# Transposing the next batch's K and Q in 512-column units, one unit per query tile, in a hard-max attention kernel

## The chip, the cores and the metric

The kernel runs on one core of one Trainium2 chip. The metric is the time of one execution on the device in microseconds (us). Every kernel here was executed several times; unless said otherwise a time is the median of those executions, with the lowest and the highest beside it. Times are compared only between executions of the same chip session and only between executions in the fast state.

The engines are named by what they do: TensorE multiplies matrices (PE in the profile, PEld for its weight loads), VectorE (DVE) does elementwise work and reductions, ScalarE (ACT) here moves results from PSUM, the memory that this kernel's matmuls write, to SBUF, where its other tiles lie (such a move is called an eviction below), GpSimd (POOL) issues gathers.

## The reference

For each of four batches, every query picks the key with the largest dot product and returns that key's row of V. There is no softmax.

```python
B, Sq, Sk, D = 4, 4096, 4096, 128        # q, k, v: float32 normal numbers

def reference(q, k, v):
    logits = np.matmul(q, k.transpose(0, 2, 1))
    best = np.argmax(logits, axis=-1)
    b_idx = np.arange(q.shape[0])[:, None]
    return v[b_idx, best, :].astype(np.float32)
```

## The kernel before

A query tile is 128 queries; there are 32 tiles a batch, 128 in all. For each tile the kernel screens groups of four keys in fp16 with a mix of sums and differences (max(a, b) = half of the sum plus half of the absolute difference), then recomputes the best groups exactly. Only the screening matters here. A tile costs:

- TensorE: 12 matmuls of 512 columns: two `pd` tiles (differences) of two, two `psn` tiles (sums) of two, and two more per `psn` that add the absolute difference `A`.
- ScalarE: three evictions of 1024 columns: `A` twice, `E` once.
- VectorE: the fold (an int16 maximum of `psn` and `E` into `W`), the top-8 search of `W`, and small work.

```python
    pp = ctx.enter_context(tc.tile_pool(name="ps", bufs=4, space=bass.MemoryType.PSUM))
    # ... cut: the four slots of this pool hold all PSUM tiles, up to 1024 fp32 columns each
    def dpart(t, x):
        # ... cut
        ps = pp.tile([P, 1024], FP32, tag="u", name=f"pd_{t}_{x}")
        mm(ps, t, 1 + 2 * x, True)
        A = ep.tile([P, 1024], FP16, tag=f"A{x}", name=f"A_{t}_{x}")
        nc.scalar.activation(out=A, in_=ps, func=AF.Abs)

    def spart(t, x):
        # ... cut
        ps = pp.tile([P, 1024], FP32, tag="u", name=f"psn_{t}_{x}")
        mm(ps, t, 2 * x, False)
        # ... cut: adds A with two matmuls by an identity
        if x == 0:
            E = ep.tile([P, 1024], I16, tag="E", name=f"E_{t}")
            nc.scalar.activation(out=E, in_=ps, func=AF.Relu)
        # ... cut: the second psn stays in PSUM for the fold

    def fold(t):
        E, ps = E_t.pop(t)
        nc.vector.tensor_tensor(out=W_t[t % NW].bitcast(I16)[:, 1::2], in0=ps, in1=E, op=OP.max)
```

While a batch runs, the K and Q of the next batch are loaded in natural order and transposed on TensorE. Each block of 1024 columns is transposed into one PSUM tile and evicted by ScalarE in one instruction. A block of K takes 16 matmuls of 128 columns, since each output is a sum or a difference of two keys' columns. A block of Q takes 8.

```python
    def trn_half(b, u, h):
        x = 2 * (u // 2)
        if h == 0:
            tk_t[u] = pp.tile([P, 1024], FP32, tag="u", name=f"tk_{b}_{u}")
        ps = tk_t[u]
        for m in range(4):
            o = ps[:, h * 512 + m:(h + 1) * 512:4]
            nc.tensor.matmul(out=o, lhsT=natk[b % 2][:, h, 4 * m + x, :], rhs=identh, start=True, stop=False)
            nc.tensor.matmul(out=o, lhsT=natk[b % 2][:, h, 4 * m + x + 1, :],
                             rhs=identn if u % 2 else identh, start=False, stop=True)
        if h == 1:
            nc.scalar.activation(out=kT[b % 2][:, u * 1024:(u + 1) * 1024], in_=ps, func=AF.Copy)
    # ... cut: trn_k calls trn_half for h = 0 and 1; trn_q is the same for Q, 8 matmuls, adjacent columns

        # the loop over tiles; qt is the tile's number in its batch
            if 2 <= qt < 10:
                load_part(b + 1, qt - 2)          # K of the next batch
            elif 14 <= qt < 22:
                load_part(b + 1, qt - 6)          # Q of the next batch
            if 18 <= qt < 22:
                trn_k(b + 1, order[qt - 18])      # one K block in each of four tiles
            if 24 <= qt < 24 + NQT // 8:
                trn_q(b + 1, qt - 24)             # one Q block in each of four tiles
            # ... cut
            if it > 0:
                screen(it)
        if 0 <= it - 1 < T:
            fold(it - 1)
        if it % NQT in (9, 13) and it < T:
            put_k(it // NQT + 1, it % NQT // 13)  # a VectorE instruction of 0.94 us, twice a batch
```

## Time and profile before

| | before |
|---|---|
| time, median of 3 (range) | 505.31 us (504.83 to 505.49) |
| profiled execution | 510.92 us, span 508.9 us |
| VectorE / TensorE / ScalarE busy | 419.9 / 402.2 / 390.3 us |
| tile with no transposes | 3.1 us |
| tile with a K block | 3.9 to 4.9 us (exceptions: 2.9 us for the first in batches 0 and 2, 5.4 us for one with flag work) |
| tile with a Q block | 3.3 to 3.7 us |

The profiled execution took 5.6 us longer than the median of the timed ones. (Flag work is a chain of short VectorE and TensorE instructions, run once for each half of the tiles, that looks for queries that need a further exact check.)

First, the page of the kernel before: the span, the busy time of each engine with its share and count, and three groups of instructions. A group's line gives busy time and mean ns of one, then the engine's idle time just before these instructions and what ended most of it.

```profile
span 508.9 us, 6436 instructions
PE 402.2 (79%) x1960; PEld 188.6 (37%) x1960; DVE 419.9 (83%) x833; ACT 390.3 (77%) x417; POOL 312.8 (61%) x345
L211 DVE TENSOR_TENSOR W<-psn,E 128x1024 int16<-128x1024 f32 x128 | 166.3, 1299 | 33.7 <-ACT E L198 23.7
L153 ACT ACTIVATE kT<-tk 128x1024 f16<-128x1024 f32 x16 | 16.3, 1026 | 23.7 <-PE tk L150 22.6
L167 ACT ACTIVATE qT<-tq 128x1024 f16<-128x1024 f32 x16 | 18.5, 1159 | 0.7 <-PE tq L165 0.7
```

VectorE is the busiest, but 83% does not say whether it is the limit. The fold line says that VectorE stood idle for 33.7 us before folds, mostly for `E` from ScalarE (10.5 us of this lie ahead of the program's first fold). The kT line says that ScalarE in turn stood idle for 23.7 us before the K evictions, waiting for the transposes.

Next, busy time by stage in the same trace: a stretch of the last batch, the K tiles of the second batch (numbered batch 1 from here on), and that batch's Q tiles.

```profile
core 0: us, PE busy (x) PEld busy (x) DVE busy (x) ACT busy (x) POOL busy (x), PEclk, DMA share, GB/s
380.00:440.00 60.00, 48.48 (x204) 19.64 (x203) 60.00 (x122) 47.86 (x51) 38.12 (x39) 0.97 0.26 74
175.00:194.00 19.00, 18.10 (x110) 11.15 (x109) 13.26 (x25) 14.91 (x16) 13.53 (x15) 1.00 0.63 108
194.00:214.00 20.00, 18.70 (x105) 8.88 (x104) 18.34 (x34) 20.00 (x24) 11.39 (x13) 1.00 0.28 67
```

Where there is nothing to transpose, VectorE is busy for all of 60.00 us, so it is the limit. In the K tiles no engine is busy all the time: VectorE 13.26 of 19 us, ScalarE 14.91, but TensorE 18.10. TensorE's own work in a K tile is 12 x 0.215 + 16 x 0.109 = 4.32 us, which is most of the tile; the rest points to a chain of waits. In the Q tiles ScalarE is busy for all of 20.00 us.

The chain in a K tile is seen on ScalarE's timeline (start, duration, then in brackets its idle time before and what ended it):

```profile
180.76 1.02 ACT L153 ACTIVATE kT<-tk 128x1024 f16<-128x1024 f32 x1 [1.08 <-issue]
181.68 1.02 ACT L185 ACTIVATE A<-pd 128x1024 f16<-128x1024 f32 x1
182.58 1.03 ACT L198 ACTIVATE E<-psn 128x1024 int16<-128x1024 f32 x1
183.49 1.04 ACT L185 ACTIVATE A<-pd 128x1024 f16<-128x1024 f32 x1
185.60 1.02 ACT L153 ACTIVATE kT<-tk 128x1024 f16<-128x1024 f32 x1 [1.08 <-PE tk L150]
```

ScalarE does four evictions about 0.905 us apart, then waits 1.08 us for the next block's transposes. 4 x 0.905 + 1.08 = 4.7 us, and the tile takes 4.84 us (185.60 - 180.76). VectorE, which needs 3.1 us, waits for the rest before its folds:

```profile
179.03 1.31 DVE L211 TENSOR_TENSOR W<-psn,E 128x1024 int16<-128x1024 f32 x1 [1.00 <-PE psn L195]
183.88 1.31 DVE L211 TENSOR_TENSOR W<-psn,E 128x1024 int16<-128x1024 f32 x1 [1.46 <-PE psn L195]
188.72 1.30 DVE L211 TENSOR_TENSOR W<-psn,E 128x1024 int16<-128x1024 f32 x1 [1.92 <-ACT E L198]
193.29 1.31 DVE L211 TENSOR_TENSOR W<-psn,E 128x1024 int16<-128x1024 f32 x1 [1.36 <-ACT E L198]
```

### The profile page before, as it was taken

The numbers are of one execution on the slowest core, as the hardware profiler recorded it, in microseconds if no ns is written. First come the engines' busy times: TensorE is split into PE (matmuls) and PEld (weight loads), VectorE is DVE, ScalarE is ACT, GpSimd is POOL, SyncE is SP. The second block draws the span as 40 slices with busy tenths as digits, with TensorE's granted clock in tenths as the row PEclk, the third lists the DMA queues.
The fourth block names the chain that finished last, engine by engine and source line by source line (L and its number), as shares of the span: only waits on it lengthen the run. The fifth ranks groups of instructions, "written<-read, shape, count | busy, mean of one in ns | idle before, by whom it ended". The sixth has DMA issues, their size and how long they took to land. (4 is left out here: it accounts for less than half of the span.)

```text
span 508.9 us, 6436 instructions
## 1 busy us (share of the span) xinstructions
PE 402.2 (79%) x1960; PEld 188.6 (37%) x1960; DVE 419.9 (83%) x833; ACT 390.3 (77%) x417; POOL 312.8 (61%) x345
## 2 busy tenths in 40 slices
PE   8999999999999799999998899999988999000000
PEld 5544455444433364444333644443333333000000
DVE  2179997999999968999999889999999999861030
ACT  1999978999998779999998699999978999000000
POOL 9124456556787876566887865576646666677430
PEclk9999999999999999999999999999999999655555
DMA  9715254232545572314554651323311313244210
GB/s 133 126 24 90 83 77 66 59 88 61 124 90 148 109 129 55 93 52 107 96 131 118 102 104 50 84 62 91 98 37 57 96 55 101 58 117 114 73 55 4
DMA packets 51751, 43.47 MB, mean 85 GB/s; under 512 B 24424, under 2 KB 45931, under 8 KB 51712
## 3 DMA queue, kind: packets, MB, share of 16 engines
q0 software_dynamic: 31520, 30.97, 30.5%
q1 hardware_dynamic: 20192, 12.06, 8.1%
q8 instruction: 15, 0.25, 0.2%
q14 instruction: 24, 0.20, 0.1%
HBM read 39.59 MB, written 12.19 MB: 102 GB/s over the span
## 5 line engine op out<-in xcount | busy, mean ns | idle before, releaser
L185 ACT ACTIVATE A<-pd 128x1024 f16<-128x1024 f32 x256 | 266.9, 1106 | 8.6 <-PE pd L176 6.7
L231 POOL DMA_INDIRECT kg<-k,cand x128 | 125.7, 982 | 128.0 <-DVE p L250 34.2
L211 DVE TENSOR_TENSOR W<-psn,E 128x1024 int16<-128x1024 f32 x128 | 166.3, 1299 | 33.7 <-ACT E L198 23.7
L176 PE MATMUL psn<-kT,qT 128*128 128x512 f16 x512 | 151.8, 378 | 23.5 <-ACT A L185 12.6
L176 PEld LDWEIGHTS <-qT 128*128 128x128 f16 x1024 | 100.0, 98 | 171.2 <-issue 79.6
L176 PE MATMUL pd<-kT,qT 128*128 128x512 f16 x512 | 152.5, 379 | 6.6 <-ACT A L185 3.0
L214 DVE MAX8 TOP<-W 128x8 f32<-128x1024 f32 x128 | 156.0, 1219 | 0.0
L195 PE MATMUL psn<-A,identh 128*128 128x512 f16 x512 | 152.1, 378 | 0.0
L281 POOL DMA_INDIRECT vr<-in_v_dram,win x128 | 126.8, 991 | 39.0 <-issue 37.2
L198 ACT ACTIVATE E<-psn 128x1024 int16<-128x1024 f32 x128 | 141.1, 1102 | 9.4 <-PE psn L195 4.1
L195 PEld LDWEIGHTS <-identh 128*128 128x128 f16 x512 | 49.6, 97 | 60.8
L246 DVE TENSOR_TENSOR prod<-kg,natq 128x768 f16<-128x768 f16 (+1 forms) x65 | 35.1, 541 | 3.0 <-DMA kg<-k,cand 3.0
L153 ACT ACTIVATE kT<-tk 128x1024 f16<-128x1024 f32 x16 | 16.3, 1026 | 23.7 <-PE tk L150 22.6
L149 PE MATMUL tk<-identh,natk 128*128 128x128 f16 x128 | 28.7, 309 | 0.2 <-issue 0.2
L250 DVE TENSOR_TENSOR p<-prod 128x384 f16<-128x384 f16 (+1 forms) x65 | 22.5, 348 | 0.0
L65 POOL DMA_DIRECT2D natq<-in_q_dram x26 | 22.3, 857 | 0.1
L255 DVE TENSOR_REDUCE D<-p 128x6 f32<-128x192 f16 (+1 forms) x65 | 21.6, 333 | 0.0
L336 PE MATMUL fp<-n,tri 128*128 128x1 f32 x4 | 0.9, 304 | 24.1 <-DVE n L332 24.1
L167 ACT ACTIVATE qT<-tq 128x1024 f16<-128x1024 f32 x16 | 18.5, 1159 | 0.7 <-PE tq L165 0.7
L150 PEld LDWEIGHTS <-natk 128*128 128x128 f16 x128 | 17.2, 134 | 2.0 <-issue 0.8
L149 PEld LDWEIGHTS <-natk 128*128 128x128 f16 x128 | 17.3, 135 | 1.5
L62 POOL DMA_DIRECT2D natk<-in_k_dram x26 | 15.7, 604 | 0.9 <-POOLq L605 0.8
(87 smaller groups left out, 168.7 us busy)
## 6 DMA issues: line engine op xcount, KB each, us to landing
out_dram<-vr SPq DMA_DIRECT2D x13, 512.0 KB
k<-kd SPq DMA_DIRECT2D x8, 384.0 KB
natk<-in_k_dram POOLq DMA_DIRECT2D x24, 128.0 KB
natq<-in_q_dram POOLq DMA_DIRECT2D x24, 128.0 KB
kg<-k,cand POOLq DMA_INDIRECT x128
vr<-in_v_dram,win POOLq DMA_INDIRECT x128
natk<-in_k_dram POOLq DMA_DIRECT2D x2, 512.0 KB
out_dram<-vr SPq DMA_DIRECT2D x4, 256.0 KB
```

The costliest lines, as they stand in the source:

```text
L65: nc.gpsimd.dma_start(out=natq[b % 2][:, x:y], in_=q[b].rearrange("(t p) d -> p t d", p=P)[:, x:y])
L149: nc.tensor.matmul(out=o, lhsT=natk[b % 2][:, h, 4 * m + x, :], rhs=identh, start=True, stop=False)
L176: nc.tensor.matmul(out=ps[:, n * 512:(n + 1) * 512], lhsT=qT[b % 2][:, qt * P:(qt + 1) * P], rhs=kT[b % 2][:, u * 1024 + n * 512:u * 1024 ...
L185: nc.scalar.activation(out=A, in_=ps, func=AF.Abs)
L195: nc.tensor.matmul(out=ps[:, n * 512:(n + 1) * 512], lhsT=identh, rhs=A[:, n * 512:(n + 1) * 512], start=False, stop=True)
L198: nc.scalar.activation(out=E, in_=ps, func=AF.Relu)
L211: nc.vector.tensor_tensor(out=W_t[t % NW].bitcast(I16)[:, 1::2], in0=ps, in1=E, op=OP.max)
L214: nc.vector.max(out=TOP[:, t, :], in_=W_t[t % NW].bitcast(FP32))
L231: near_q.append(lambda j=j: nc.gpsimd.indirect_dma_start(out=kg[:, j].rearrange("p f d -> p (f d)"), out_offset=None, in_=k16[t0 // NQT], ...
L246: nc.vector.tensor_tensor(out=prod, in0=kg, in1=natq[b % 2][:, x - b * NQT:x - b * NQT + m, :].unsqueeze(2).to_broadcast([P, m, 3, P]), op ...
L250: nc.vector.tensor_tensor(out=p1, in0=prod[:, :, :, 0:64], in1=prod[:, :, :, 64:128], op=OP.add)
L281: late_q.append(lambda j=j: nc.gpsimd.indirect_dma_start(out=vr[:, j, :], out_offset=None, in_=v_flat, in_offset=IOA(ap=win[:, j:j + 1], a ...
```

## The change

The intent: cut the eight blocks of a batch into 16 units of 512 columns, each with its own PSUM tile and its own eviction, and give each of 16 consecutive tiles one unit (K in tiles 10 to 17, Q in 18 to 25). ScalarE then never waits for 16 transposes at once, and no tile carries a full fourth eviction. The arithmetic and the number of matmuls stay the same; 24 evictions are added. The Q loads move two tiles earlier. The first batch's own transposes at the start stay as they were.

```diff
--- before.py
+++ after.py
@@ -152,10 +152,22 @@
         if h == 1:
             nc.scalar.activation(out=kT[b % 2][:, u * 1024:(u + 1) * 1024], in_=ps, func=AF.Copy)
 
-    def trn_k(b, u):
-        if b < B:
-            trn_half(b, u, 0)
-            trn_half(b, u, 1)
+    def unit_k(b, u, h):
+        x = 2 * (u // 2)
+        ps = pp.tile([P, 512], FP32, tag="u", name=f"uk_{b}_{u}_{h}")
+        for m in range(4):
+            o = ps[:, m::4]
+            nc.tensor.matmul(out=o, lhsT=natk[b % 2][:, h, 4 * m + x, :], rhs=identh, start=True, stop=False)
+            nc.tensor.matmul(out=o, lhsT=natk[b % 2][:, h, 4 * m + x + 1, :],
+                             rhs=identn if u % 2 else identh, start=False, stop=True)
+        nc.scalar.activation(out=kT[b % 2][:, u * 1024 + h * 512:u * 1024 + (h + 1) * 512], in_=ps, func=AF.Copy)
+
+    def unit_q(b, g):
+        ps = pp.tile([P, 512], FP32, tag="u", name=f"uq_{b}_{g}")
+        for i in range(4):
+            nc.tensor.matmul(out=ps[:, i * P:(i + 1) * P], lhsT=natq[b % 2][:, g * 4 + i, :], rhs=identh,
+                             start=True, stop=True)
+        nc.scalar.activation(out=qT[b % 2][:, g * 512:(g + 1) * 512], in_=ps, func=AF.Copy, scale=QSCALE)
 
     def trn_q(b, g):
         if b >= B:
@@ -482,7 +494,6 @@
     cuts = list(range(0, T - 24 + 1, 8)) + [T - x for x in (20, 16, 12, 8, 6, 4, 2, 1, 0)]
     chunks = list(zip(cuts[:-1], cuts[1:]))
     SEGS = [0, T // 2, T]
-    order = (1, 0, 3, 2)
     live = []
 
     def start(g, kind):
@@ -550,12 +561,13 @@
             b, qt = it // NQT, it % NQT
             if 2 <= qt < 10:
                 load_part(b + 1, qt - 2)
-            elif 14 <= qt < 22:
-                load_part(b + 1, qt - 6)
-            if 18 <= qt < 22:
-                trn_k(b + 1, order[qt - 18])
-            if 24 <= qt < 24 + NQT // 8:
-                trn_q(b + 1, qt - 24)
+            elif 12 <= qt < 20:
+                load_part(b + 1, qt - 4)
+            if b + 1 < B:
+                if 10 <= qt < 18:
+                    unit_k(b + 1, qt % 4, (qt - 10) // 4)
+                elif 18 <= qt < 26:
+                    unit_q(b + 1, qt - 18)
             if it in (2, 4, 6):
                 trn_q(0, it // 2)
             if it > 0:
```

## The prediction

> **What bounds it now.** By the page, VectorE is busy 83% of the 508.9 us span, ScalarE 77%, TensorE 79%. The stage decides. In a window from 380 to 440 us, in the last batch, which has no next batch to transpose, VectorE is busy 60.00 of 60 us: a query tile costs 3.1 us there. ScalarE needs 2.7 us a tile (three evictions, 0.905 us apart in the timeline), TensorE 2.6 us (12 matmuls of 512 columns, 0.215 us apart). The main loop is VectorE-bound, except where the next batch is transposed. There the timeline and the gaps before the folds (the int16 max into W) show:
> - K: four tiles a batch take 3.9-4.9 us. ScalarE waits about 1.08 us for the 16 transposes (1.70 us of TensorE, 0.106 us each) and has a fourth eviction: 4 x 0.905 + 1.08 = 4.7 us. VectorE idles 3.3, 5.7 and 3.3 us in the three batches.
> - Q: four tiles take 3.3-3.7 us (four evictions, 3.62 us). VectorE idles 1.7, 1.7 and 1.3 us.
> Together 17 us: all that the change can win.
>
> **What the change does.** 8 blocks a batch become 16 units, one a tile: K in tiles 10-17, Q in 18-25. Arithmetic and transposes stay. Added: 24 evictions. [...] A 512-column tile occupies a whole slot of the four, as before. In the K tiles of the new program order three slots rotate through ScalarE and the fold keeps the fourth, which is better than before. Q loads move two tiles earlier; six tiles (19 us) remain before use.
>
> **New cost, per tile.**
> - K unit: TensorE 2.6 + 8 x 0.106 + about 0.1 of start = 3.55 us, ScalarE 2.7 + 0.48 = 3.2, VectorE 3.1. These tiles become TensorE-bound, at 3.55-3.6. Eight lose 3.6 us a batch against VectorE; it enters with about 0.8 us of slack, so 2.8-3 us. In batch 2 flag work makes VectorE slower there: about 1.5.
> - Q unit: ScalarE 3.2 us against VectorE 3.05: 1.2 us a batch.
> New idle time: 4.2 + 4.2 + 2.7 = 11 us, in place of 17. Gain about 5 us, all on the critical path: only VectorE's idle time moves. The tail (60 us) and the start stay.
>
> **Predicted:** 500.5 us; 8 times in 10 between 496.5 and 504.5. Faster by over 2%: 0.09; within 2%: 0.89; slower by over 2%: 0.02.
>
> **To check in the profile.** VectorE's busy time unchanged (419.9 us), its idle time before the fold down by some 6 us; fold spacing 3.5-3.6 us in the K tiles (4.6 before), 3.2 in the Q tiles (3.67 before); K evictions wait under 0.3 us for TensorE (1.0-1.5 before); 512-column evictions spaced 0.45-0.5 us; ScalarE's instructions 417 to 441; nobody waits for natq loads.
>
> **What would make it wrong.** If TensorE runs further ahead than I think, K tiles stay VectorE-bound and the gain nears 12-15 us. If a short eviction costs 0.7 us, or in the Q tiles, where the second pd waits for the previous fold's slot, this closes a loop longer than 3.2 us, the gain goes to zero: 16 tiles a batch would each lose 0.4 us. If Q loads land late, TensorE stalls.

The forecast's sum: with 0.48 us, the estimate, it came to 3.2 us of ScalarE in a tile with a unit, to 11 us of idle time in place of 17 and to 500.5 us. The trace of before shows 0.905 us for 1024 columns, half of which is 0.45 us; the trace of after then showed 0.48 us for Q units and 0.49 us for K units. The 0.1 us of start in a K unit, the 0.8 us of slack and the 1.5 us in batch 2 are estimates too. Of the start the trace of before shows 0.05 us: two `psn` matmuls start at 183.18 us and fill 2 x 0.215 us, to 183.61, and the first transpose starts at 183.66.

## The result, and the profile after

| | before | after |
|---|---|---|
| time, median of 4 (range) | 505.08 us (504.83 to 505.49) | 499.99 us (499.54 to 500.47) |
| ratio, 95% interval | | 0.9898 (0.9881 to 0.9916): within 2% |
| VectorE / TensorE / ScalarE busy | 419.9 / 402.2 / 390.3 us | 420.5 / 399.9 / 394.5 us |
| ScalarE instructions | 417 | 441 |
| tile with K work (batch 0) | 2.9 to 4.6 us, four tiles | 3.1 to 3.6 us, eight tiles; 3.46 us on average over the last five |
| tile with Q work (batch 0) | up to 3.7 us, four tiles | 3.23 us on average, eight tiles |

A ratio here and below is the mean time of one kernel's fast runs over that of the other's of the same rounds, so it is not quite the ratio of the medians quoted. The changed kernel is correct.

The same lines of the page of the changed kernel:

```profile
span 498.3 us, 6462 instructions
PE 399.9 (80%) x1960; PEld 187.9 (38%) x1960; DVE 420.5 (84%) x833; ACT 394.5 (79%) x441; POOL 310.7 (62%) x345
L223 DVE TENSOR_TENSOR W<-psn,E 128x1024 int16<-128x1024 f32 x128 | 166.5, 1301 | 25.5 <-ACT E L210 16.4
L163 ACT ACTIVATE kT<-uk 128x512 f16<-128x512 f32 x24 | 14.6, 606 | 4.2 <-PE uk L161 3.5
L170 ACT ACTIVATE qT<-uq 128x512 f16<-128x512 f32 x24 | 17.1, 710 | 0.9 <-PE uq L168 0.9
```

The wait of K evictions for TensorE has nearly gone: 4.2 us before 24 unit evictions. (The 16 of the kernel before include four at the start of the program, which the changed kernel still does in blocks, with 9.6 us of waiting that nothing changed.) VectorE's busy time is the same. Only its idle time moved, from 33.7 us before folds to 25.5 us.

Busy time by stage: seven of the eight K tiles, and seven of the eight Q tiles, of batch 0.

```profile
core 0: us, PE busy (x) PEld busy (x) DVE busy (x) ACT busy (x) POOL busy (x), PEclk, DMA share, GB/s
49.50:73.10 23.60, 23.60 (x139) 13.70 (x137) 22.21 (x36) 22.86 (x29) 10.25 (x12) 1.00 0.51 93
73.10:95.70 22.60, 20.81 (x116) 9.75 (x114) 21.41 (x36) 22.60 (x29) 14.81 (x16) 1.00 0.36 65
```

Now each stage has one limiting engine. In the K tiles TensorE is busy for all of 23.60 us, in the Q tiles ScalarE for all of 22.60 us. ScalarE and the folds in the K tiles:

```profile
60.07 0.60 ACT L163 ACTIVATE kT<-uk 128x512 f16<-128x512 f32 x1
60.56 1.02 ACT L197 ACTIVATE A<-pd 128x1024 f16<-128x1024 f32 x1
61.48 1.02 ACT L210 ACTIVATE E<-psn 128x1024 int16<-128x1024 f32 x1
62.39 1.03 ACT L197 ACTIVATE A<-pd 128x1024 f16<-128x1024 f32 x1
63.53 0.60 ACT L163 ACTIVATE kT<-uk 128x512 f16<-128x512 f32 x1
```

```profile
55.80 1.31 DVE L223 TENSOR_TENSOR W<-psn,E 128x1024 int16<-128x1024 f32 x1 [0.36 <-PE psn L207]
59.27 1.31 DVE L223 TENSOR_TENSOR W<-psn,E 128x1024 int16<-128x1024 f32 x1 [0.25 <-PE psn L207]
62.88 1.30 DVE L223 TENSOR_TENSOR W<-psn,E 128x1024 int16<-128x1024 f32 x1
66.20 1.31 DVE L223 TENSOR_TENSOR W<-psn,E 128x1024 int16<-128x1024 f32 x1
69.66 1.31 DVE L223 TENSOR_TENSOR W<-psn,E 128x1024 int16<-128x1024 f32 x1 [0.63 <-PE psn L207]
73.12 1.31 DVE L223 TENSOR_TENSOR W<-psn,E 128x1024 int16<-128x1024 f32 x1
```

The 512-column eviction holds ScalarE for 0.49 us from its start to the next start (60.07 to 60.56). The folds are (73.12 - 55.80) / 5 = 3.46 us apart. One tile takes 3.61 us (59.27 to 62.88) because VectorE has its put_k instruction of 0.94 us there, and the next 3.32 us: TensorE went on meanwhile, so that tile lost nothing.

TensorE's timeline shows what it does with the time. The unit's matmuls start 0.11 us apart, each writing every fourth PSUM column:

```profile
62.64 0.31 PE L160 MATMUL uk<-identh,natk 128*128 128x128 f16 x1
62.75 0.31 PE L161 MATMUL uk<-identn,natk 128*128 128x128 f16 x1
```

12 x 0.215 + 8 x 0.109 = 3.45 us: the whole K tile.

**Where the time came from.** I added up VectorE's gaps between the first fold of batch 0 and the first of batch 3, from the traces. The last batch has none in any of them.

| trace | idle in batches 0 / 1 / 2 | sum | first fold | last fold | after the last fold |
|---|---|---|---|---|---|
| before, first trace (510.92 us) | 11.0 / 7.4 / 4.7 | 23.1 | 20.9 | 436.8 | 72.1 |
| before, second trace (504.53 us) | 11.0 / 5.5 / 4.1 | 20.7 | 20.6 | 434.0 | 68.5 |
| after (500.26 us) | 8.7 / 2.6 / 3.9 | 15.1 | 20.8 | 429.6 | 68.7 |

Against the second trace of before, 5.5 us of idle time went and the last fold comes 4.3 us earlier. (VectorE's busy time was 1.0 us lower in that trace, 419.5 us, and the first fold 0.2 us earlier; this closes the sum.) After the last fold the two are equal. The first trace of before makes the gain look like 10.6 us, but 3.4 us of that lie after the last fold, which the change doesn't touch, and some 2 us in batch 1. Those belong to that execution and not to the kernel.

### The profile page after: what moved, and what is told of

The parts are those of the page before. It is cut to its first block, busy times and chain, and to the rows that moved or that the text cites. A ratio compares the mean times of both kernels' runs of the same rounds, so it can differ in the third digit from the quotient of the medians.

```text
span 498.3 us, 6462 instructions
## 1 busy us (share of the span) xinstructions
PE 399.9 (80%) x1960; PEld 187.9 (38%) x1960; DVE 420.5 (84%) x833; ACT 394.5 (79%) x441; POOL 310.7 (62%) x345
## 5 line engine op out<-in xcount | busy, mean ns | idle before, releaser
L243 POOL DMA_INDIRECT kg<-k,cand x128 | 124.1, 970 | 123.3 <-DVE p L262 30.7
L223 DVE TENSOR_TENSOR W<-psn,E 128x1024 int16<-128x1024 f32 x128 | 166.5, 1301 | 25.5 <-ACT E L210 16.4
L210 ACT ACTIVATE E<-psn 128x1024 int16<-128x1024 f32 x128 | 138.0, 1078 | 7.8 <-PE psn L207 7.1
L160 PE MATMUL uk<-identh,natk 128*128 128x128 f16 x96 | 22.2, 303 | 0.0
L163 ACT ACTIVATE kT<-uk 128x512 f16<-128x512 f32 x24 | 14.6, 606 | 4.2 <-PE uk L161 3.5
L170 ACT ACTIVATE qT<-uq 128x512 f16<-128x512 f32 x24 | 17.1, 710 | 0.9 <-PE uq L168 0.9
L265 DVE TENSOR_TENSOR p<-p 128x192 f16<-128x192 f16 (+1 forms) x65 | 16.1, 250 | 0.0
```

The costliest lines, as they stand in the source:

```text
L243: near_q.append(lambda j=j: nc.gpsimd.indirect_dma_start(out=kg[:, j].rearrange("p f d -> p (f d)"), out_offset=None, in_=k16[t0 // NQT], ...
```

## The experiments

The theory: a tile takes as long as its busiest engine or its longest chain. The block made a chain of 4.7 us in K tiles and four full evictions in Q tiles; the unit replaces them by a TensorE limit (K) and a smaller ScalarE limit (Q), and that exchange is the gain. (The 4.7 us is not the whole story of the K tiles before: TensorE's 4.32 us is nearly as long. This is taken up under e0.) The first rival: the gain comes from the place of the work in the batch, which changed too (K from tiles 18-21 to 10-17, Q from 24-27 to 18-25, the Q loads two tiles earlier), not from how it is cut. The second rival: the slow trace of before is typical, and the gain partly chance.

The first four kernels ran on one chip, five rounds each, beside 9 runs of the kernel before: 504.46 us (504.27 to 504.93).

### e0: the kernel before, unchanged

No edit.

> The kernel before, unchanged, for a second trace and for the noise. Its first profiled execution took 510.9 us where the timed ones took 505, and its trace lost 10.6 us against the changed kernel where the times lost 5.1. Expected: ratio 1.000 within 0.002; if the profile is ordinary this time (about 505), its main loop (first fold to last fold) is about 2 us shorter than in the first trace and the tail after the last fold about 3 us shorter; the four K tiles still take 4.4 to 4.9 us.

Measured: 504.64 us (504.53 to 504.99), ratio 1.0003 (0.9989 to 1.0016). So the noise of such a comparison is some 0.1%, against the 1.0% of the change. It also gave the second trace. The fold line of its page:

```profile
L211 DVE TENSOR_TENSOR W<-psn,E 128x1024 int16<-128x1024 f32 x128 | 168.1, 1313 | 30.9 <-ACT E L198 25.5
```

30.9 us of idle time before folds in place of 33.7: the last two K tiles of every batch still take 4.34 to 4.85 us, so the loss is real, but the first trace overstated it in batch 1. The second rival falls.

This trace also shows what limits the K tiles of the kernel before. The last two of batch 0 take 4.56 and 4.34 us (columns as in the stages above):

```profile
77.90:86.80 8.90, 8.90 (x57) 5.76 (x56) 6.13 (x11) 7.31 (x9) 5.84 (x7) 1.00 0.45 66
```

TensorE is busy for all of 8.90 us, and the starts of its matmuls leave no more than 0.08 us of idle time in the two tiles. So here TensorE sets the pace already before the change. In other K tiles, such as the one of 4.85 us in batch 1, TensorE idles for 0.46 us, and there the chain adds to its work. Most of what a K block costs is therefore TensorE's 16 x 0.109 us, and this work stays. What changes is the number of tiles that it can hide in: in a tile without transposes TensorE needs some 0.5 us less than VectorE (3.1 - 12 x 0.215), so four more tiles hide some 2 us more a batch. This is an estimate; the K tiles of batches 0 and 1 lost 3.3 and 3.9 us before and lose 1.55 and 1.58 us after. The chain is the smaller part, and no run sets the two fully apart (e3 comes nearest).

### e1: whole blocks, only moved earlier

```diff
-            elif 14 <= qt < 22:
-                load_part(b + 1, qt - 6)
-            if 18 <= qt < 22:
-                trn_k(b + 1, order[qt - 18])
-            if 24 <= qt < 24 + NQT // 8:
-                trn_q(b + 1, qt - 24)
+            elif 12 <= qt < 20:
+                load_part(b + 1, qt - 4)
+            if 14 <= qt < 18:
+                trn_k(b + 1, order[qt - 14])
+            if 22 <= qt < 22 + NQT // 8:
+                trn_q(b + 1, qt - 22)
```

> Whole blocks of 1024 as before, only moved to earlier tiles (K in tiles 14-17, Q in 22-25, Q loads where the changed kernel has them). Theory (cost of one tile: a whole K block makes ScalarE wait for 16 transposes and evict a fourth time, 4.6 to 4.7 us against 3.1 of VectorE): the place does not matter, 504 to 506 us. Rival (the gain comes from the new place and the earlier loads, with another order of PSUM slots): about 500 us.

Measured: 502.44 us (501.98 to 502.46), ratio 0.9955 (0.9941 to 0.9968). This is a miss. The place alone gains 2.0 us, some 40% of what the change gains, and the first rival is partly right. In the traces VectorE's idle time in batches 0 to 2 falls from 20.7 to 18.8 us. The Q tiles of batches 0 and 1 lose 1.30 us a batch in place of 1.66, and the K tiles of batch 1 lose 3.2 in place of 3.9, while those of batch 0 still lose 3.3. The move also widened the distance between the last K and the first Q block from two free tiles to four, in which ScalarE and TensorE can get ahead of VectorE again. It changed which PSUM slot each tile takes, moved the Q loads, put the first K block into a tile with put_k, and moved the blocks away from the flag work of batch 2. Which of these does it was not tested.

### e2: whole blocks, every second tile

```diff
-            if 18 <= qt < 22:
-                trn_k(b + 1, order[qt - 18])
-            if 24 <= qt < 24 + NQT // 8:
-                trn_q(b + 1, qt - 24)
+            if 14 <= qt < 22 and qt % 2 == 0:
+                trn_k(b + 1, order[(qt - 14) // 2])
+            if 22 <= qt < 30 and qt % 2 == 0:
+                trn_q(b + 1, (qt - 22) // 2)
```

The Q loads are moved as in e1.

> Whole blocks of 1024, one every second tile (K 14,16,18,20, Q 22,24,26,28). Theory: what matters is the excess of a tile over VectorE that the lead of the other engines cannot cover; between two blocks there is now a tile in which TensorE (2.6 us) regains about 0.45 us of lead on VectorE (3.1 us). K loses 1.1 us a block in place of 1.4, Q about 0.1 in place of 0.4: about 500 to 501 us, close to the changed kernel although nothing is halved. Rival (the halved unit with its own PSUM tile is what gains): 504 to 505 us.

Measured: 501.6 us (501.44 to 502.12), ratio 0.9941 (0.9927 to 0.9954): a little short of what was expected. In batch 0 three K block tiles cost 4.00, 3.99 and 3.76 us, and the tiles between them are VectorE-bound again. So spreading alone helps, but a block is too long to be made up in one tile: TensorE needs 4.32 + 2.58 = 6.9 us for the two, VectorE some 6.2, and from 65.66 to 84.03 us TensorE is busy for 18.07 of 18.37 us.

### e3: units, but two in one tile

The changed kernel's units, in the places of e1's blocks.

```diff
-                if 10 <= qt < 18:
-                    unit_k(b + 1, qt % 4, (qt - 10) // 4)
-                elif 18 <= qt < 26:
-                    unit_q(b + 1, qt - 18)
+                if 14 <= qt < 18:
+                    for h in range(2):
+                        unit_k(b + 1, (1, 0, 3, 2)[qt - 14], h)
+                elif 22 <= qt < 26:
+                    for h in range(2):
+                        unit_q(b + 1, 2 * (qt - 22) + h)
```

> Units of 512 with their own PSUM tiles, but two in one tile, so the same work per tile as a whole block (K 14-17, Q 22-25). Theory: a K tile is then bound by TensorE, 2.6 + 16 x 0.106 = 4.3 us plus about 0.1, in place of 4.6 to 4.7 (the first eviction overlaps the second half's transposes); a Q tile by ScalarE, 2.7 + 2 x 0.49 = 3.7 us in place of 3.67. About 503 us (502 to 504.5). Rival (small units with their own tile give the whole gain): about 500 us.

Measured: 501.16 us (500.99 to 501.59), ratio 0.9935 (0.9921 to 0.9948). The time expected was missed, since it left out the gain of the place; against e1, in the same places, it is 1.3 us faster. Three K tiles of batch 0 take 3.46, 4.34 and 4.34 us (12 x 0.215 + 16 x 0.109 = 4.32, so the "about 0.1" expected on top is not there) where e1's take 4.07, 4.34 and 4.34; in both, TensorE is busy throughout these three tiles. Ahead of them it stands idle once in e1, for 0.46 us, and not in e3. So in batch 0 the cut takes away a wait of TensorE, not its work. Full Q tiles take 3.62 to 3.78 us (e1: 3.67).

So the 5.1 us divide roughly like this: moved earlier 2.0 us (e1), each block cut in two 1.3 us (e3), one unit per tile the rest, some 1.8 us (the changed kernel's 0.9898 of 504.46 is 499.3). The last step changes places again, so the division is not exact.

The next four ran on a chip that was disturbed throughout: the kernel before took 510.36 us there (507.98 to 512.75), and its traces show single stalls of 1 to 2 us that no wait explains (in a0 TensorE stands idle for 1.18 us ahead of 163.73 us, and the trace names no releaser). Their cause stays open. What the traces say of single tiles is still of use; differences of a per cent are not.

### a0: the changed kernel again

No edit.

> The changed kernel again, to stand beside the next kernels on the same chip. 499.5 to 500.3 us, ratio 0.990 within 0.002.

Measured: ratio 0.9926 (0.9887 to 0.9965), from a median of 508.4 us with one of six runs slow (which the ratio leaves out); the 499.5 to 500.3 us expected were missed on this chip. The gain has the same sign and about the same size; the interval is too wide for more.

### e4: one unit every second tile

```diff
             if b + 1 < B:
-                if 10 <= qt < 18:
-                    unit_k(b + 1, qt % 4, (qt - 10) // 4)
-                elif 18 <= qt < 26:
-                    unit_q(b + 1, qt - 18)
+                if 10 <= qt < 26 and qt % 2 == 0:
+                    unit_k(b + 1, (qt - 10) // 2 % 4, (qt - 10) // 8)
+                elif 26 <= qt and qt % 2 == 0:
+                    unit_q(b + 1, (qt - 26) // 2)
+            if 0 < b and qt < 10 and qt % 2 == 0:
+                unit_q(b, 3 + qt // 2)
```

The last five Q units are done in the batch that uses them, ahead of their use. (One superfluous Q unit is done at the very end; nothing uses it.)

> The same 16 units, but one every second tile: K in tiles 10 to 24, Q in 26, 28, 30 and in tiles 0 to 8 of its own batch. Theory (what counts is the excess of a tile over VectorE that the lead of TensorE and ScalarE does not cover): the excess of a K unit over VectorE is 0.35 us on TensorE, that of a Q unit 0.15 us on ScalarE, and the tile between them wins back 0.4, so VectorE has no idle time left in the K and Q tiles (now 2.6, 2.6 and 3.9 us in the three batches, of which some 1.5 us in the third belong to other work). 493 to 495 us. Rival (each unit costs its work wherever it stands): as the changed kernel, 500.

Measured on the disturbed chip: 502.45 us (500.34 to 505.95), ratio 0.9859 (0.9821 to 0.9897). The direction is clear, the size was not; so it was repeated on a quiet chip (with 9 runs of the kernel before at 504.71 us, 504.04 to 505.5).

> The units every second tile again, because the chip of the first run was disturbed (the kernel before took 508 to 513 us there, and stalls of 1 to 2 us that the trace gives to no releaser fell into both traces; e4 came out at 0.986 and the changed kernel at 0.993 of before). On a quiet chip, where before takes about 505: 493 to 496 us, ratio 0.977 to 0.983, and VectorE idle in the K tiles of batch 0 under 0.5 us in all.

Measured: 497.16 us (497.02 to 497.40), ratio 0.9849 (0.9836 to 0.9862). It is faster than the changed kernel, which agrees with the theory that a unit's cost can be hidden in the free tile after it; in batch 0 the first K units cost VectorE nothing. But it misses the 493 to 496 us expected. In batch 0 only 0.7 us of idle time is left in the K tiles, also a little more than expected; in batches 1 and 2 it is still 2.6 and 4.1 us. Most of the latter lies in one tile of 5.5 us that carries flag work.

### e5: half the K matmuls (wrong result)

```diff
-            nc.tensor.matmul(out=o, lhsT=natk[b % 2][:, h, 4 * m + x, :], rhs=identh, start=True, stop=False)
-            nc.tensor.matmul(out=o, lhsT=natk[b % 2][:, h, 4 * m + x + 1, :],
-                             rhs=identn if u % 2 else identh, start=False, stop=True)
+            nc.tensor.matmul(out=o, lhsT=natk[b % 2][:, h, 4 * m + x, :], rhs=identh, start=True, stop=True)
```

> The changed kernel with one transpose in place of the accumulating pair (wrong result on purpose: sum and difference of two K rows are not formed). Half of TensorE's work in a K unit, everything else alike. Theory (K tiles are TensorE-bound): fold spacing in undisturbed K tiles falls from 3.46 to ScalarE's 3.24 us. Rival (K tiles bound by ScalarE or by slots): stays 3.46. Only tile spacings are read, the data-dependent end may differ.

Measured: one look on the disturbed chip, 501.76 us, whose total says nothing. Folds in the K tiles of batch 0:

```profile
62.11 1.29 DVE L221 TENSOR_TENSOR W<-psn,E 128x1024 int16<-128x1024 f32 x1
65.22 1.29 DVE L221 TENSOR_TENSOR W<-psn,E 128x1024 int16<-128x1024 f32 x1
68.14 1.31 DVE L221 TENSOR_TENSOR W<-psn,E 128x1024 int16<-128x1024 f32 x1
71.45 1.30 DVE L221 TENSOR_TENSOR W<-psn,E 128x1024 int16<-128x1024 f32 x1
```

They are (71.45 - 62.11) / 3 = 3.11 us apart; the same three tiles of the changed kernel are (73.12 - 62.88) / 3 = 3.41 us apart. Idle time in the K tiles falls from 1.55 to 0.27 us. The busy time of four of these tiles:

```profile
58.88:71.83 12.95, 12.73 (x66) 6.22 (x65) 12.85 (x22) 12.95 (x17) 7.12 (x9) 1.00 0.65 103
```

ScalarE is now busy for all of 12.95 us, and its four evictions repeat every 12.95 / 4 = 3.24 us: the limit has moved to ScalarE, as expected, and VectorE draws on its lead. Less TensorE work and the same ScalarE work: so the K tile of the changed kernel is TensorE-bound, in batch 0. In batch 1 the proof is weaker: 0.97 of 1.58 us of idle time stays there, on a disturbed chip.

### e7: transposes into adjacent PSUM columns, sorted out by ScalarE

```diff
-            o = ps[:, m::4]
+            o = ps[:, m * P:(m + 1) * P]
...
-        nc.scalar.activation(out=kT[b % 2][:, u * 1024 + h * 512:u * 1024 + (h + 1) * 512], in_=ps, func=AF.Copy)
+        nc.scalar.activation(out=kT[b % 2][:, u * 1024 + h * 512:u * 1024 + (h + 1) * 512].rearrange("p (j m) -> p m j", m=4),
+                             in_=ps.rearrange("p (m j) -> p m j", m=4), func=AF.Copy)
```

> K units as in the changed kernel, but the four transposes of a unit write 128 adjacent PSUM columns each and the eviction puts them at every fourth column of kT instead. A K transpose is spaced 0.106 us (it writes every fourth PSUM column, in pairs that accumulate), a Q transpose about 0.055 to 0.06 (adjacent columns, no pairs). If the stride is the reason, K transposes go to about 0.06 us, TensorE needs 3.1 us in a K tile and the tile is bound by ScalarE at about 3.24: about 497.5 us if the strided eviction is as fast as now (0.49 us). If the pairs are the reason, spacing stays 0.106 and K tiles 3.46. If the strided eviction is slower than 0.8 us, K tiles get longer and the time is over 500.

Measured: correct, 513.04 us (510.27 to 514.14), ratio 1.0038 (1.0006 to 1.007), on the disturbed chip. The transposes start 0.055 us apart in place of 0.109, so the strided PSUM output was half of their cost. But ScalarE's eviction, which now writes every fourth fp16 in SBUF, got slow. ScalarE's timeline in a K tile:

```profile
57.19 1.90 ACT L163 ACTIVATE kT<-uk 128x512 f16<-128x512 f32 x1
58.23 1.70 ACT L198 ACTIVATE A<-pd 128x1024 f16<-128x1024 f32 x1
...
61.07 1.89 ACT L163 ACTIVATE kT<-uk 128x512 f16<-128x512 f32 x1
```

The durations shown overlap here, so starts are compared: from its start to the next start it is 1.04 us (57.19 to 58.23) where the contiguous eviction takes 0.49. The tile takes 3.88 us (61.07 - 57.19), now bound by ScalarE, which has no gap. The stride was moved from one engine to another and cost more there.

The last three ran on a quiet chip together with e4_again above.

### e6: short evictions in batches 2 and 3 (wrong result)

Only the units made for batches 2 and 3 are shortened, so what happens during batches 1 and 2 is read.

```diff
+        n = 64 if b > 1 else 512
-        nc.scalar.activation(out=kT[b % 2][:, u * 1024 + h * 512:u * 1024 + (h + 1) * 512], in_=ps, func=AF.Copy)
+        nc.scalar.activation(out=kT[b % 2][:, u * 1024 + h * 512:u * 1024 + h * 512 + n], in_=ps[:, 0:n], func=AF.Copy)
... the same in unit_q
```

> The changed kernel with evictions of 64 columns in place of 512 for the units of batches 2 and 3 (wrong result on purpose; the transposes stay; units of batch 1 unchanged for comparison). [...] Theory: Q tiles are ScalarE-bound at 3.24 us, so during batches 1 and 2 they become VectorE-bound (mean about 3.05, no idle time), while K tiles stay at TensorE's 3.46 to 3.6. Rival (Q tiles bound by the slot that the fold keeps): Q tiles stay at 3.24.

Measured: the wrong keys sent the kernel into its slow exact path, and the total of 3515.86 us means nothing. The tiles of batch 1 come ahead of that. In its Q tiles the folds are

```profile
180.58 1.30 DVE L225 TENSOR_TENSOR W<-psn,E 128x1024 int16<-128x1024 f32 x1
183.42 1.28 DVE L225 TENSOR_TENSOR W<-psn,E 128x1024 int16<-128x1024 f32 x1
...
195.57 1.30 DVE L225 TENSOR_TENSOR W<-psn,E 128x1024 int16<-128x1024 f32 x1 [0.15 <-PE psn L209]
198.89 1.30 DVE L225 TENSOR_TENSOR W<-psn,E 128x1024 int16<-128x1024 f32 x1
```

(198.89 - 180.58) / 6 = 3.05 us apart in place of 3.23, with 0.4 us of idle time in place of some 1.0. In the K tiles the two longest waits stay: 0.60 and 0.44 us, in the changed kernel 0.76 and 0.44 (a third, of 0.25 us, goes). So a Q tile is bound by ScalarE and a K tile mostly isn't; with e5, each limit is shown by taking away its cause, that of the K tiles in batch 0 and that of the Q tiles in batch 1.

### e8: adjacent PSUM columns, and a contiguous eviction

e7 showed the transposes to be half as dear when they write adjacent columns. The order of keys within a block doesn't matter to the screening, as long as the index that is carried in the low 16 bits of `W` follows it. So the keys stay in the order in which they come, and the index code, which is made once, is permuted:

```diff
-            o = ps[:, m::4]
+            o = ps[:, m * P:(m + 1) * P]
...
-            o = ps[:, h * 512 + m:(h + 1) * 512:4]
+            o = ps[:, h * 512 + m * P:h * 512 + (m + 1) * P]
...
-        nc.gpsimd.iota(out=W.bitcast(U16)[:, 0::2], pattern=[[-1, NG]], base=NG - 1, channel_multiplier=0)
+        nc.gpsimd.iota(out=W.bitcast(U16)[:, 0::2].rearrange("p (h m j) -> p h m j", h=2, m=4),
+                       pattern=[[-512, 2], [-1, 4], [-4, 128]], base=NG - 1, channel_multiplier=0)
```

> The changed kernel with each K transpose written to 128 adjacent PSUM columns (0.055 us apart in the run with the strided eviction, against 0.109), the eviction left contiguous too (0.49 us), and the new column order put right in the index code under W (one other iota pattern); batch 0's start does the same. Right result expected. If K tiles are TensorE-bound in the changed kernel (3.46 us), they become ScalarE-bound at 3.24 now, as with one transpose per pair. The start saves up to 64 x 0.05 = 3 us of TensorE, of which I expect half to show. 496 to 498 us. If the stride was not what cost the time: 499 to 500.

Measured: correct, 493.94 us (493.62 to 494.54), ratio 0.9787 (0.9773 to 0.98). This is better than expected. TensorE's timeline in a unit:

```profile
59.80 0.22 PE L162 MATMUL uk<-identn,natk 128*128 128x128 f16 x1
59.85 0.22 PE L161 MATMUL uk<-identh,natk 128*128 128x128 f16 x1
```

They start 0.055 us apart, and idle time in the K tiles falls to 0.27, 0.46 and 0.24 us in the three batches (1.55, 1.58 and 1.63 in the changed kernel). Another 1.9 us come from the start of the program, where batch 0's own transposes got shorter: the first fold starts at 18.85 us in place of 20.77.

### e9: both, e8 with one unit every second tile

The edits of e4 and e8 together.

> Both: adjacent PSUM columns and one unit every second tile. VectorE should have no idle time in the K and Q tiles at all, and the start is shorter: 490 to 493 us, ratio 0.972 to 0.977, faster than every other kernel here. If the two do not add up, about as the better of the two.

Measured: correct, 489.8 us (489.47 to 489.95), ratio 0.9702 (0.9689 to 0.9716): 3% faster than the kernel before, the fastest kernel, and a little better than expected. Busy time in its stage of K and Q work of batch 0:

```profile
47.60:93.50 45.90, 45.69 (x244) 21.04 (x243) 45.90 (x79) 45.90 (x55) 25.88 (x28) 1.00 0.46 83
```

(The columns are as in the stages above: TensorE, weight loads, VectorE, ScalarE, GpSimd.) VectorE is busy for all of 45.90 us there: the transposes of the next batch cost it nothing in batch 0. (ScalarE and TensorE show 45.90 and 45.69 us too, so a full busy time alone does not name the limit; that needs a run such as e5 or e6.) The idle time summed over batches 0 to 2 as above:

| kernel | profiled execution | idle time, batches 0-2 | first fold | last fold |
|---|---|---|---|---|
| before (e0) | 504.53 us | 20.7 us | 20.6 us | 434.0 us |
| e1 | 502.44 us | 18.8 us | 20.6 us | 431.8 us |
| e2 | 502.12 us | 17.6 us | 21.2 us | 431.6 us |
| e3 | 501.14 us | 17.8 us | 20.6 us | 430.8 us |
| after | 500.26 us | 15.1 us | 20.8 us | 429.6 us |
| e4_again | 497.10 us | 13.6 us | 20.6 us | 426.6 us |
| e8 | 493.83 us | 11.5 us | 18.9 us | 423.3 us |
| e9 | 489.62 us | 8.6 us | 18.9 us | 419.1 us |

Measured from the first row, the time follows VectorE's idle time to within 1.3 us once the start of the first fold is counted. Of e9's remaining 8.6 us, 4.0 lie in the first three tiles of batch 0, and 1.9 in one tile of batch 2 that takes 4.84 us; so its expectation of no idle time at all holds in batch 0 alone.

## Why the prediction was right

The time on record was 500.5 us with a range of 496.5 to 504.5; 499.99 us was measured. The gain predicted was 505.31 - 500.5 = 4.8 us, the gain measured 505.08 - 499.99 = 5.1 us. Point by point:

- **What bounds the kernel.** Right for the plain tiles: VectorE (60.00 of 60 us busy). In the K tiles only in part: the prediction named a chain through ScalarE of 4.7 us, but TensorE's own 4.32 us is most of it, and in the last two K tiles of batch 0 TensorE is busy throughout (8.90 of 8.90 us, e0). That mainly VectorE's idle time would move is shown by the last table, to within 1.3 us.
- **K tiles become TensorE-bound, Q tiles ScalarE-bound.** Right, and shown for the K tiles of batch 0 by e5 and for the Q tiles of batch 1 by e6, which take away one engine's work each, and by the stages (TensorE 23.60 of 23.60 us, ScalarE 22.60 of 22.60).
- **A 512-column eviction takes about 0.48 us.** Right: 0.49 us for K units (60.07 to 60.56) and 0.48 us for Q units (86.46 to 86.94). An estimate from the two spacings that the traces show, 0.905 us for 1024 columns and 0.49 us for 512: (0.905 - 0.49) / 512 = 0.81 ns a column, and 0.49 us less 512 x 0.81 ns leaves 0.075 us an eviction.
- **"Together 17 us: all that the change can win."** Too large. These 17 us were read from a trace of before that was 5.6 us slower than the kernel's timed executions; the difference was in the table of times, and the prediction did not use it. In the second, ordinary trace it is 14.6 us in the same tiles.
- **"Eight lose 3.6 us a batch against VectorE ... so 2.8-3 us."** Too large in batches 0 and 1, which lose 1.55 and 1.58 us; for batch 2 it said about 1.5, and 1.63 was measured. Two terms were off. The tile takes 3.46 us, not 3.55: the "about 0.1 of start", an estimate, does not exist, as TensorE has no gap in these tiles in batch 0. And the comparison took VectorE's tile as 3.1 us throughout, while two of the eight tiles have put_k and keep VectorE busy for 3.61 us, in which TensorE catches up.
- **Q tiles lose 1.2 us a batch.** About right: 1.06 and 0.99 us in batches 0 and 1. In batch 2 it is 2.2 us, 1.5 of them in one tile of flag work.
- **Idle time 17 to 11 us.** It went from 14.6 to 9.1 us. Both terms were too large by about 2 us, and their difference came out nearly right: 5.5 us against 6. By batch it was 2.6, 2.6 and 3.9 us after, where 4.2, 4.2 and 2.7 were predicted: too large in the first two, too small in the third, where the flag work costs more. The total is so close in part because errors cancel, and that is luck.
- **Waits of K evictions under 0.3 us.** Right: at most 0.12 us in batch 0, and 0.20 to 0.23 us in batches 1 and 2. Nobody waits for the Q loads, as predicted.
- **The way of the PSUM slots** (three rotate through ScalarE, the fold keeps the fourth). This was read from the program's order. The trace doesn't contradict it, but in batches 1 and 2 some K tiles take 3.6 to 3.88 us, and there `psn` waits for ScalarE (0.17 us for `A` in batch 1, 0.21 to 0.23 us for the K eviction in batch 2), and no run tested the slots by themselves.

What the prediction did not see at all: moving the unchanged blocks four and two tiles earlier gains 2.0 us by itself (e1). It ascribed the whole gain to cutting the blocks. That the place matters is shown; why it does is only argued.

It also took the 0.106 us of a transpose as given. e7 and e8 show that half of it is the price of writing every fourth PSUM column (0.109 us from start to start against 0.055), and removing that stride is worth more than the change itself (e8 493.94 us against the changed kernel's 0.9898 x 504.71 = 499.6).

## What to carry to other kernels

In this kernel, work for the next stage that is interleaved with a loop cost what it added to the limiting engine of the tile it sat in, less the slack that the other engines had there and in the tiles next to it. So cut such work to pieces, spread them over more tiles, and leave a free tile between pieces if one piece still makes another engine the limit (e4, e9). Add up each engine's work in a tile before you call a wait a chain: the engine that is waited for may simply be full, as TensorE was here. And before you schedule such work around, ask whether its unit price is right: here a layout change that cost one permuted index table halved the time of the transposes (0.109 to 0.055 us from start to start), and e9, which adds it and the spread to the cut, gained 14.9 us over the kernel before where the change gained 5.1. And compare the time of the profiled execution with the timed ones before you sum up idle time from its trace; here the trace overstated what could be won by 2.4 us.
